# A hybrid SSM and convolution layer: SSM readout put into token order once by ScalarE, readout tables in three buffers, six weight low halves on VectorE

## The chip, the cores and the metric

The kernel runs on one core of a Trainium2 chip. The metric is device time in microseconds (us) of one execution, as the median of several executions. The engines are named as in the profile: PE is TensorE, PEld its weight load, DVE is VectorE, ACT is ScalarE, POOL is GpSimd, SP is the SyncE queue that issues most of the transfers.

## The reference

One layer of a diffusion backbone over 1024 latent tokens of 1024 channels, with a prefix of 256 context tokens. Cut to what the change touches:

```
p   = modulate(rmsnorm(x, norm1_g), sh1, sc1) @ w_in        # 512 SSM, 3 x 512 conv, 2 x 1024 gate columns
y   = d_skip * u + sum over 2 directions of Re(C @ states)  # S5 diagonal SSM, 32 groups of 16 channels, 64 states
z   = gelu(y)
y_a = z * sigmoid(z @ glu_w + glu_b)                        # GLU, 512 x 512
merged = sigmoid(p_a) * (y_a @ proj_a) + sigmoid(p_b) * (y_b @ proj_b)
x   = x + g1 * (merged @ w_out)
x   = x + g2 * conv_ffn(modulate(rmsnorm(x, norm2_g), sh2, sc2))   # g1, sh2, sc2, g2 from silu(c) @ mod_w
out = rmsnorm(x, final_g)
```

All tensors are float32.

## The kernel before

The large matrix products are made of three matmuls each: both operands are cut into a high half (a copy rounded to the PE's fp32r type) and a low half (operand minus high half), and high x high, low x high and high x low are summed in PSUM. `weight(src, lo_eng)` (L190) loads a weight tile of 128x1024 into `raw` (two buffers), ACT writes its high half `whi`, and `lo_eng`, POOL where `pool_e` is passed and DVE otherwise, writes the low half `wlo`. `split` (L205) does the same for activations: ACT the high half, DVE the low half. Each product that fills a 128x1024 PSUM tile is 48 matmuls of 128x512 for the gates (`gate_matmul`, key `ga` or `gb`) and 24 for the projections and the GLU (`proj_matmul`, keys `pa`, `pb`, `glu`). The PSUM tiles of this stretch rotate through two buffers, and ACT (a sigmoid, `sggb` or `sgga`) or DVE (`mb`, `sgga`) empties them.

The SSM works on chunks of 8 tokens: 128 latent chunks. Its readout for a pair of groups (`readout(sb)`, 16 of them) loads a table of three 128x128 matrices per group from `Yd` and the inputs of the two groups from `Ud` into one tile `wt` of two buffers, copies the chunk states out of `XS` into `S2` (ACT the upper 64 partitions, DVE the lower 64), multiplies, applies gelu into `Zt`, and stores `Zt` to `Zd`. `Zd` then holds z with the token index split as (place in the chunk j, chunk c). Four tiles `z[m]` are loaded from it in that order, 128 x 8 x 128. The high and low halves that the GLU and proj_a read are written in token order, so each `split` of a `z[m]` writes with a step of eight elements; the GLU's product with its sigmoid is done with the sigmoid read at that step.

Around the readouts run `branch_b(d)`, a gate `gb` and a product `pb` for each of 8 column blocks d. Then come the gate `ga0`, the four GLU products, and for each d a gate `ga` and a product `pa`. In the same stretch DVE works off 32 dot products for the second modulation (`mod_cols(n)`, tile `mw`, two buffers of 512 KB loads, result in `modc`), whose end the last scaled `w_out` tile and the norm of the second half wait for. Two small stores of `modc` columns (`mod_row`, into `rowd`) are in the SP queue as well.

The program is written once, and a scheduler orders the instructions of each engine ahead of time. Each engine, the SP queue too, works its list strictly in that order. A tile pool with n buffers lets the n+1st tile start only when the first one's last reader is done.

Of the kernel before, what the change touches and what calls it, by code (L numbers as in the profile page):

```python
# [13 lines left out]
F32 = mybir.dt.float32  # L14
# [3 lines left out]
AF = mybir.ActivationFunctionType  # L18
ALU = mybir.AluOpType
# [3 lines left out]
P = 128  # L23
D = 1024
SEQ = 1024
# [7 lines left out]
MS = SW // P  # L33
G = 32
H = 16
L = 8
NCC = CTX // L
NCL = SEQ // L
# [117 lines left out]
def layer_kernel(es: ExitStack, tc, I, out):  # L156
    nc = tc.nc
    sync, act, dve, pool_e, pe = nc.sync, nc.scalar, nc.vector, nc.gpsimd, nc.tensor

    def pool(name, bufs=1, stack=es, **kw):  # L160
        return stack.enter_context(tc.tile_pool(name=name, bufs=bufs, **kw))
# [17 lines left out]
    def ax_tile(shape, key):  # L179
        return psum["ax"].tile(shape, F32, name=f"ax_{key}", tag="ax")  # L180
# [3 lines left out]
    hold = {}  # L184

    def held(eng):
        ins = hold.get(eng)
        return tc.issue_after(ins.ins) if ins is not None else nullcontext()

    def weight(src, lo_eng=None, wpool=wp, scale=None):  # L190
        i = cnt["w"]
        cnt["w"] += 1
        raw = wp.tile([P, D], F32, name=f"raw{i}", tag="raw", bufs=2)
        sync.dma_start(raw, src)
        if scale is not None:
            dve.tensor_tensor(raw, raw, scale, op=ALU.mult)  # L196
        hi = wpool.tile([P, D], F32R, name=f"whi{i}", tag="whi")
        with held("act"):
            act.activation(hi, raw, AF.Copy)  # L199
        lo = wpool.tile([P, D], F32R, name=f"wlo{i}", tag="wlo")  # L200
        with held("dve") if lo_eng is None else nullcontext():
            (lo_eng or dve).tensor_tensor(lo, raw, hi.bitcast(F32), op=ALU.subtract)  # L202
        return hi, lo

    def split(hi, lo, src):  # L205
        act.activation(hi, src, AF.Copy)  # L206
        return dve.tensor_tensor(lo, src, hi.bitcast(F32), op=ALU.subtract)  # L207
# [23 lines left out]
    Ud = dram.tile([SW, L, NC], F32, name="Ud")  # L231
    NSB = G // 2
    Zd = dram.tile([MS, P, L, NCL], F32, name="Zd")
    Yd = dram.tile([NSB, P, 2, 3, P], F32, name="Yd")
# [168 lines left out]
    s, c = sm.sincos(sm.tt(li, dt, ALU.mult))  # L403
# [288 lines left out]
    conv = {}  # L692
# [80 lines left out]
    def ytile(key, m):  # L773
        return (yp.tile([P, SEQ], F32R, name=f"{key}h{m}", tag=f"yh{m}"),
                yp.tile([P, SEQ], F32R, name=f"{key}l{m}", tag=f"yl{m}"))
# [13 lines left out]
    rd = pool("rd", bufs=2, stack=es_x)  # L789

    def readout(sb):
        g0 = sb * 2
        wt = rd.tile([P, 2, 4, P], F32, name=f"wt{sb}", tag="wt")
        sync.dma_start(wt[:, :, 0:3, :], Yd[sb])
        sync.dma_start(wt[:, :, 3, :],
                       Ud[g0 * H:(g0 + 2) * H, :, NCC:].rearrange("(g h) j c -> (h j) g c", h=H))
        S2 = rd.tile([P, 2, 2, NCL], F32, name=f"S2{sb}", tag="S2")
        for i in range(2):
            src = XS[:, NCC - 1:NC - 1, i, g0:g0 + 2].rearrange("p s g -> p g s")
            act.activation(S2[0:64, i], src[0:64], AF.Copy)  # L800
            dve.tensor_copy(S2[64:128, i], src[64:128, :, ::-1])
        py = ax_tile([P, 2, NCL], f"Y{sb}")
        for g in range(2):
            pe.matmul(py[:, g, :], wt[:, g, 0, :], S2[:, 0, g, :], start=True, stop=False)
            pe.matmul(py[:, g, :], wt[:, g, 1, :], S2[:, 1, g, :], start=False, stop=False)
            pe.matmul(py[:, g, :], wt[:, g, 2, :], wt[:, g, 3, :], start=False, stop=True)
        Zt = rd.tile([P, 2, NCL], F32, name=f"Zt{sb}", tag="Zt")
        act.activation(Zt, py, AF.Gelu_apprx_tanh)
        for g in range(2):
            m, q = divmod(g0 + g, 8)  # L810
            sync.dma_start(Zd[m][q * H:(q + 1) * H].rearrange("h i c -> i h c"), Zt[:, g, :])

    def proj_matmul(wt, d, rh, rl, key):
        ps = mm_tile(key)
        hi, lo = wt
        for n in range(2):
            sl = slice(n * HALF, (n + 1) * HALF)
            for k in range(MS):
                ks = slice((d * MS + k) * P, (d * MS + k + 1) * P)
                mm3(ps[:, sl], (hi[:, ks], lo[:, ks]), (rh[k][:, sl], rl[k][:, sl]), k == 0, k == MS - 1)  # L820
        return ps

    def gate(m, key):
        psg = gate_matmul(m, key, None if 24 <= m < 28 else pool_e)
        sg = sgp.tile([P, SEQ], F32, name=f"sg{key}", tag="sg")
        act.activation(sg, psg, AF.Sigmoid)
        return sg
# [9 lines left out]
    for d, n in enumerate((0, 6, 6, 4)):  # L837
        branch_b(d)
        for q in range(n):
            readout(nread + q)  # L840
        nread += n
# [5 lines left out]
    mb += [mbt[1][:, d, :] for d in range(KT - MA)]  # L847
    es_z = ExitStack()
    zp = pool("zp", stack=es_z)
    z = [zp.tile([P, L, NCL], F32, name=f"z{m}") for m in range(MS)]  # L850
    for m in range(MS):
        sync.dma_start(z[m], Zd[m])
    es_md = ExitStack()
    md = pool("md", bufs=2, stack=es_md, side="right")
    sc2 = md.tile([P, D], F32, name="sc2", bufs=1)
# [3 lines left out]
    def mod_cols(n):  # L859
        mw = md.tile([P, D], F32, name=f"mw{n}", tag="mw")  # L860
        sync.dma_start(mw, I["mod_wT"][n * P:(n + 1) * P, :])
        with held("y"):
            dve.tensor_tensor_reduce(out=mw, in0=mw, in1=sc2, scale=1.0, scalar=0.0, op0=ALU.mult, op1=ALU.add,  # L863
                                     accum_out=modc[:, n:n + 1])
# [11 lines left out]
    def ysplit(key):  # L876
        hi, lo = [], []
        for m in range(MS):
            h, l_ = ytile(key, m)
            hold["y"] = split(h.rearrange("p (c j) -> p j c", j=L), l_.rearrange("p (c j) -> p j c", j=L), z[m])  # L880
            hi.append(h)
            lo.append(l_)
        return hi, lo

    zh, zl = ysplit("z")
    sgd = {0: gate(16, "ga0")}
    NM = 16 + 9 + 6
    for n in range(16 + 9, NM):
        mod_cols(n)
    for m in range(MS):  # L890
        if m % 2 == 0:
            wt = weight(I["glu_w"][m // 2], pool_e)
        ps = proj_matmul(wt, m % 2, zh, zl, f"glu{m}")
        sg = zp.tile([P, SEQ], F32, name=f"sgz{m}", tag="sgz", bufs=1)
        act.activation(sg, ps, AF.Sigmoid, bias=glub[:, m:m + 1])
        dve.tensor_tensor(z[m], z[m], sg.rearrange("p (c j) -> p j c", j=L), op=ALU.mult)
    yah, yal = ysplit("ya")

    def mod_done(a, b):
# [14 lines left out]
    def load_wout(k, src):  # L914
        raw = (wo.tile([P, D], F32, name=f"raw_o{k}", tag="xr", bufs=2) if k < 3 else
               wp.tile([P, D], F32, name=f"raw_o{k}", tag="raw", bufs=2))
        sync.dma_start(raw, I["w_out"][k * P:(k + 1) * P, :])
        (dve if k < 3 else pool_e).tensor_tensor(raw, raw, g1b, op=ALU.mult)
        hi, lo = (src.tile([P, D], F32R, name=f"wo{t}{k}", 
                          **({"tag": "sg"} if src is sgp else {"tag": f"y{t}{k % MS}", "bufs": 1})) for t in ("h", "l"))  # L920
        split(hi, lo, raw)
        wout.append((hi, lo))

    for d in range(KT):
        if d + 1 < KT:
            sgd[d + 1] = gate(17 + d, f"ga{d + 1}")
        if d % 2 == 0:
            wt = weight(I["proj_a"][d // 2], pool_e)
        ps = proj_matmul(wt, d % 2, yah, yal, f"pa{d}")
        sg = sgd.pop(d)  # L930
        dve.tensor_tensor(sg, ps, sg, op=ALU.mult)
        pool_e.tensor_tensor(mb[d], mb[d], sg, op=ALU.add)
        for n in range(NM + 5 * (d - 1), min(48, NM + 5 * d)) if d else ():
            mod_cols(n)
        if 2 <= d < 4:
            load_wout(d - 2, wo)
        if d == 5:
            es_md.close()
            md = pool("md2", stack=es_g, side="right")
            load_wout(2, md)  # L940
# [5 lines left out]
    op = pool("op", bufs=2, stack=es_o)  # L946
# [81 lines left out]
    f = [fp.tile([P, SEQ], F32, name=f"f{k}") for k in range(KF)]  # L1028
# [183 lines left out]
```

## Time and profile before

| what | value |
|---|---|
| runs, us | 1459.26, 1464.06, 1464.45 |
| median of the three, us | 1464.06 |
| profiled execution, own time, us | 1457.23 |
| profiled execution, span, us | 1455.4 |
| PE busy in the span | 1399.7 us (96%) |
| DVE, ACT, POOL busy | 979.1, 535.2, 477.5 us |
| granted PE clock over the span, mean | 0.987 |

The profiled execution is a little faster than the three timed ones; 1.8 us of its own time lie outside the span. Matmuls are pipelined, so a matmul's duration is longer than the distance to the next one, and PE counts as busy also while it works at its lower clock. The readouts lie between 354 and 421 us of the span, the GLU between 458 and 487, and the gates and products with proj_a reach to about 617.

### The profile page before, as it was taken

The page shows a single profiled execution, that of the slowest core. Times are in us where ns is not written, and L with a number is a line of the kernel's source. Part 1 is how long each engine was busy: PE and PEld are TensorE (multiplying, and loading weights), DVE is VectorE, ACT ScalarE, POOL GpSimd, SP SyncE. Part 2 cuts the span into 40 slices and gives each one's busy share as a digit, 9 for nine tenths or more (in the row PEclk, how much of TensorE's full clock was granted, in tenths as well). Part 3 has the DMA queues.
Part 4 walks back from the last instruction along what each step waited for, and adds up shares of the span by engine and source line. Part 5 has one row for each costly group of instructions (what it writes and reads, how often), then busy time and mean ns, then how long its engine had stood idle before and what let it go on. Part 6 is the DMA issues. An engine that isn't in the chain of part 4 may idle for free. (4 is left out here: it accounts for less than half of the span.)

```text
span 1455.4 us, 16944 instructions
## 1 busy us (share of the span) xinstructions
PE 1399.7 (96%) x6488; PEld 1144.0 (79%) x6488; DVE 979.1 (67%) x1424; ACT 535.2 (37%) x758; POOL 477.5 (33%) x211
## 2 busy tenths in 40 slices
PE   6999989999899999999999999999999999998997
PEld 4788877788787777878888888888888887887885
DVE  6865859888227782147568877877878886349555
ACT  5643772223434411135433332332332342324332
POOL 0000000002101334340055465465465465635453
PEclk9999999999989999999999999999999999999998
DMA  9613212512677474143111111111111115424331
GB/s 323 208 52 96 80 57 74 143 44 87 191 236 164 154 236 103 32 143 108 71 45 58 44 46 57 44 47 55 44 50 52 44 58 188 145 87 156 100 106 58
DMA packets 82577, 148.71 MB, mean 102 GB/s; under 512 B 22336, under 2 KB 51264, under 8 KB 82496
## 3 DMA queue, kind: packets, MB, share of 16 engines
q1 hardware_dynamic: 79616, 137.90, 31.1%
q10 hardware_dynamic: 2880, 9.73, 1.9%
q8 instruction: 51, 0.84, 0.2%
q14 instruction: 30, 0.25, 0.1%
HBM read 129.80 MB, written 19.90 MB: 103 GB/s over the span
## 5 line engine op out<-in xcount | busy, mean ns | idle before, releaser
L202 POOL TENSOR_TENSOR wlo<-raw,whi 128x1024 fp32r<-128x1024 f32 x108 | 269.8, 2502 | 758.6 <-ACT whi L199 750.9
L1052 DVE SCALAR_TENSOR_TENSOR acc<-mm_up,cw,acc 128x945 f32<-128x945 f32 (+2 forms) x308 | 375.0, 1223 | 100.4 <-POOL acc L1044 91.6
L199 ACT ACTIVATE whi<-raw 128x1024 fp32r<-128x1024 f32 x126 | 133.6, 1060 | 535.4 <-issue 192.5
L213 PE MATMUL mm_up<-h2hi,wlo 128*128 128x512 f32 x704 | 274.0, 389 | 0.5 <-POOL wlo L202 0.5
L211 PE MATMUL mm_up<-h2hi,whi 128*128 128x512 f32 x704 | 273.7, 389 | 0.4 <-DVE h2hi L987 0.4
L212 PE MATMUL mm_up<-h2lo,whi 128*128 128x512 f32 x704 | 274.1, 389 | 0.0
L213 PEld LDWEIGHTS mm_up<-h2hi,wlo 128*128 128x128 f32 x704 | 132.2, 188 | 28.2 <-POOL wlo L202 0.9
L211 PEld LDWEIGHTS mm_up<-h2hi,whi 128*128 128x128 f32 x704 | 132.1, 188 | 27.9 <-DVE h2hi L987 0.7
L212 PEld LDWEIGHTS mm_up<-h2lo,whi 128*128 128x128 f32 x704 | 132.2, 188 | 27.6
L211 PE MATMUL mm_dn<-whi,fhd 128*128 128x512 f32 x308 | 119.5, 392 | 6.0 <-DVE x1r L1140 4.5
L212 PE MATMUL mm_dn<-wlo,fhd 128*128 128x512 f32 x308 | 120.6, 392 | 2.5 <-POOL wlo L202 2.5
L213 PE MATMUL mm_dn<-whi,fld 128*128 128x512 f32 x308 | 120.2, 391 | 0.0
L1044 POOL TENSOR_TENSOR acc<-acc,side 128x960 f32<-128x960 f32 x44 | 100.4, 2281 | 0.0
L207 DVE TENSOR_TENSOR fld<-f,fhd 128x512 fp32r<-128x512 f32 x44 | 58.6, 1347 | 52.4 <-ACT fhd L206 52.4
L863 DVE CUSTOM_DVE_ANT_0 mw<-mw,sc 128x1024 f32<-128x1024 f32 x32 | 54.2, 1706 | 43.0 <-DMA mw<-in_mod_wT_dram 25.5
L211 PEld LDWEIGHTS mm_dn<-whi,fhd 128*128 128x128 f32 x308 | 58.2, 189 | 19.0 <-DVE x1r L1140 4.9
L212 PEld LDWEIGHTS mm_dn<-wlo,fhd 128*128 128x128 f32 x308 | 58.3, 189 | 15.3 <-POOL wlo L202 3.5
L213 PEld LDWEIGHTS mm_dn<-whi,fld 128*128 128x128 f32 x308 | 58.1, 189 | 12.1
L196 DVE TENSOR_TENSOR raw<-raw,g2b 128x1024 f32<-128x1024 f32 x22 | 42.8, 1947 | 34.9 <-DMA raw<-in_ffn_w_down_dram 34.9
L1063 POOL TENSOR_TENSOR f<-f,acc 128x1024 f32<-128x1024 f32 x22 | 53.3, 2424 | 10.0 <-DVE acc L1052 10.0
L213 PE MATMUL mm_ga<-hhi,wlo 128*128 128x512 f32 x128 | 50.7, 396 | 4.1 <-POOL wlo L202 4.1
L213 PE MATMUL mm_o<-woh,ml 128*128 128x512 f32 x128 | 50.8, 398 | 1.1 <-DVE ml L207 1.1
(324 smaller groups left out, 2646.8 us busy)
## 6 DMA issues: line engine op xcount, KB each, us to landing
raw<-in_ffn_w_up_dram SPq DMA_DIRECT2D x44, 512.0 KB
raw<-in_ffn_w_down_dram SPq DMA_DIRECT2D x44, 512.0 KB
mw<-in_mod_wT_dram SPq DMA_DIRECT2D x32, 512.0 KB
raw<-in_w_in_dram SPq DMA_DIRECT2D x28, 512.0 KB
wt<-Yd SPq DMA_DIRECT2D x16, 384.0 KB
mt<-in_mod_wT_dram SPq DMA_DIRECT2D x8, 512.0 KB
mn<-in_mod_nat_dram SPq DMA_DIRECT2D x8, 512.0 KB
Yd<-W SPq DMA_DIRECT2D x16, 256.0 KB
```

Source lines behind the costliest of these rows:

```text
L196: dve.tensor_tensor(raw, raw, scale, op=ALU.mult)
L199: act.activation(hi, raw, AF.Copy)
L202: (lo_eng or dve).tensor_tensor(lo, raw, hi.bitcast(F32), op=ALU.subtract)
L207: return dve.tensor_tensor(lo, src, hi.bitcast(F32), op=ALU.subtract)
L211: pe.matmul(ps, lh, rh, start=first, stop=False)
L212: pe.matmul(ps, lh, rl, start=False, stop=False)
L213: pe.matmul(ps, ll, rh, start=False, stop=last)
L863: dve.tensor_tensor_reduce(out=mw, in0=mw, in1=sc2, scale=1.0, scalar=0.0, op0=ALU.mult, op1=ALU.add, accum_out=modc[:, n:n + 1])
L1044: pool_e.tensor_tensor(acc[:, 1:, :], acc[:, 1:, :], side[:, 1:, :], op=ALU.add)
L1052: dve.scalar_tensor_tensor(acc[:, r0:r1, c0:c1], u[:, r0 + dr:r1 + dr, c0 + dc:c1 + dc], cw[:, m, i:i + 1], acc[:, r0:r1, c0:c1], op0=ALU. ...
L1063: pool_e.tensor_tensor(f[k], f[k], v, op=ALU.mult)
```

## The change

```diff
     def readout(sb):
         g0 = sb * 2
-        wt = rd.tile([P, 2, 4, P], F32, name=f"wt{sb}", tag="wt")
-        sync.dma_start(wt[:, :, 0:3, :], Yd[sb])
-        sync.dma_start(wt[:, :, 3, :],
-                       Ud[g0 * H:(g0 + 2) * H, :, NCC:].rearrange("(g h) j c -> (h j) g c", h=H))
+        wt = rd.tile([P, 2, 3, P], F32, name=f"wt{sb}", tag="wt", bufs=3)
+        sync.dma_start(wt, Yd[sb])
+        if sb % 2 == 0:
+            ut = rd.tile([P, 4, NCL], F32, name=f"ut{sb}", tag="ut")
+            sync.dma_start(ut, Ud[g0 * H:(g0 + 4) * H, :, NCC:].rearrange("(g h) j c -> (h j) g c", h=H))
+            conv["ut"] = ut
+        ut = conv["ut"]
...
-            pe.matmul(py[:, g, :], wt[:, g, 2, :], wt[:, g, 3, :], start=False, stop=True)
+            pe.matmul(py[:, g, :], wt[:, g, 2, :], ut[:, sb % 2 * 2 + g, :], start=False, stop=True)
...
-    z = [zp.tile([P, L, NCL], F32, name=f"z{m}") for m in range(MS)]
+    z = [zp.tile([P, SEQ], F32, name=f"z{m}") for m in range(MS)]
     for m in range(MS):
-        sync.dma_start(z[m], Zd[m])
+        zj = zp.tile([P, L, NCL], F32, name=f"zj{m}", tag="zj", bufs=2)
+        sync.dma_start(zj, Zd[m])
+        act.activation(z[m].rearrange("p (c j) -> p j c", j=L), zj, AF.Copy)
...
-            hold["y"] = split(h.rearrange("p (c j) -> p j c", j=L), l_.rearrange("p (c j) -> p j c", j=L), z[m])
+            hold["y"] = split(h, l_, z[m])
...
-            wt = weight(I["glu_w"][m // 2], pool_e)
+            wt = weight(I["glu_w"][m // 2])
...
-        dve.tensor_tensor(z[m], z[m], sg.rearrange("p (c j) -> p j c", j=L), op=ALU.mult)
+        dve.tensor_tensor(z[m], z[m], sg, op=ALU.mult)
...
-            wt = weight(I["proj_a"][d // 2], pool_e)
+            wt = weight(I["proj_a"][d // 2])
```

The table of a readout is now one contiguous run per partition and has three buffers; the inputs come for two readouts at once in a tile of their own with two buffers. The four z tiles are loaded into `zj` (two buffers) and copied by ACT into token order, after which every reader reads and writes them in one run. The low halves of two GLU and four proj_a weight tiles go from POOL to DVE. No matmul is added or removed.

The scheduler's order changes with it. On PE, before, 115 matmuls of 128x512 lie between the first matmul of the first readout and the last of the last; now there are 68, and the last readout stands ahead of `pb5` instead of inside `gb6`, so that 216 matmuls follow it up to the GLU, where before 168 did.

In the SP queue, the end of the readouts before. `wt` rows with Yd load a table, those with Ud the inputs of the same readout; Zd rows store a result, in two transfers each:

```order
L794 DMA wt13_3380<-Yd_90 128x2x384
L795 DMA wt13_3380<-Ud_88 128x2x128
L811 DMA Zd_89<-Zt11_3274 8x16x128 x2
L794 DMA wt14_3399<-Yd_90 128x2x384
L795 DMA wt14_3399<-Ud_88 128x2x128
L811 DMA Zd_89<-Zt12_3376 8x16x128 x2
L794 DMA wt15_3418<-Yd_90 128x2x384
L811 DMA Zd_89<-Zt13_3395 8x16x128 x2
L795 DMA wt15_3418<-Ud_88 128x2x128
```

The same place in the SP queue now, `ut` being the inputs for two readouts:

```order
L794 DMA wt11_3260<-Yd_90 128x768
L814 DMA Zd_89<-Zt8_3218 8x16x128 x2
L794 DMA wt12_3361<-Yd_90 128x768
L797 DMA ut12_3363<-Ud_88 128x4x128
L814 DMA Zd_89<-Zt9_3236 8x16x128 x2
L794 DMA wt13_3381<-Yd_90 128x768
L814 DMA Zd_89<-Zt10_3256 8x16x128 x2
L794 DMA wt14_3399<-Yd_90 128x768
```

The table of readout n stood behind the store of readout n-2 or n-3; it now stands behind that of n-4, and inputs no longer stand behind a store that is needed for nothing in front of them.

On ACT, what follows the last readout before (`Zt15` is its gelu, `sc2` the silu of c for the dot products, `zh` the high halves for the GLU):

```order
L808 ACTIVATE Zt15_3433<-ax_Y15_3426 128x256
L199 ACTIVATE whi29_3741<-raw29_3739 128x1024
L826 ACT_TABLE_LOAD
L826 ACTIVATE sggb6_3699<-mm_gb6_3650 128x1024
L857 ACT_TABLE_LOAD
L857 ACTIVATE sc2_3457<-sc2_3457 128x1024
L199 ACTIVATE whi30_3856<-raw30_3854 128x1024
L826 ACT_TABLE_LOAD
L826 ACTIVATE sggb7_3794<-mm_gb7_3745 128x1024
L206 ACTIVATE zh0_3838<-z0_3446 128x8x128
```

And on ACT now:

```order
L811 ACT_TABLE_LOAD
L811 ACTIVATE Zt15_3433<-ax_Y15_3426 128x256
L199 ACTIVATE whi28_3711<-raw28_3709 128x1024
L857 ACTIVATE z0_3446<-zj0_3450 128x8x128
L857 ACTIVATE z1_3447<-zj1_3453 128x8x128
L862 ACT_TABLE_LOAD
L862 ACTIVATE sc2_3465<-sc2_3465 128x1024
L857 ACTIVATE z2_3448<-zj2_3456 128x8x128
L857 ACTIVATE z3_3449<-zj3_3459 128x8x128
L199 ACTIVATE whi29_3749<-raw29_3747 128x1024
L829 ACT_TABLE_LOAD
L829 ACTIVATE sggb6_3707<-mm_gb6_3658 128x1024
```

The four copies into token order, and the silu among them, stand ahead of the high half `whi29` that `gb7` multiplies with and of the sigmoid `sggb6` that empties the PSUM buffer into which `gb7` is summed.

On DVE, around the low halves `zl` for the GLU before (an ISA row is a dot product, or the read of its sum):

```order
L863 ISA mw24_3828,modc_82<-mw24_3828,sc2_3457 128x1024
L863 ISA modc_82 128x1
L207 TENSOR_TENSOR zl0_3839<-z0_3446,zh0_3838 128x8x128
L834 TENSOR_TENSOR mb1_3442<-mm_pb7_3796,sggb7_3794 128x1024
L207 TENSOR_TENSOR zl1_3843<-z1_3447,zh1_3842 128x8x128
L207 TENSOR_TENSOR zl2_3847<-z2_3448,zh2_3846 128x8x128
L207 TENSOR_TENSOR zl3_3851<-z3_3449,zh3_3850 128x8x128
L863 ISA mw25_3911,modc_82<-mw25_3911,sc2_3457 128x1024
```

And on DVE now, with the first GLU low half `wlo31` that POOL had:

```order
L868 ISA mw24_3836,modc_82<-mw24_3836,sc2_3465 128x1024
L868 ISA modc_82 128x1
L207 TENSOR_TENSOR zl0_3847<-z0_3446,zh0_3846 128x1024
L837 TENSOR_TENSOR mb1_3442<-mm_pb7_3804,sggb7_3802 128x1024
L207 TENSOR_TENSOR zl1_3851<-z1_3447,zh1_3850 128x1024
L207 TENSOR_TENSOR zl2_3855<-z2_3448,zh2_3854 128x1024
L202 TENSOR_TENSOR wlo31_3941<-raw31_3937,whi31_3939 128x1024
L207 TENSOR_TENSOR zl3_3859<-z3_3449,zh3_3858 128x1024
```

The same nine dot products are ahead of `zl0` as before; the four low halves keep their places, in one run each, with a weight's low half among them.

## Rows read from the trace of the kernel before

**Rows 1.** The page, part 1: busy time, share of the span, instructions.
```profile
PE 1399.7 (96%) x6488; PEld 1144.0 (79%) x6488; DVE 979.1 (67%) x1424; ACT 535.2 (37%) x758; POOL 477.5 (33%) x211
```

**Rows 2.** Windows: length, busy us (instructions) per engine, granted clock, DMA share, GB/s.
```profile
395.00:400.00 5.00, 2.24 (x18) 2.08 (x19) 1.11 (x2) 1.43 (x3) 1.60 (x1) 1.00 0.84 248
400.00:410.00 10.00, 9.02 (x39) 7.89 (x38) 2.41 (x6) 4.29 (x9) 0.00 (x0) 0.51 0.60 166
420.00:455.00 35.00, 35.00 (x154) 28.67 (x154) 14.20 (x19) 18.47 (x14) 7.15 (x3) 1.00 0.71 226
461.70:468.50 6.80, 5.91 (x14) 3.70 (x13) 5.64 (x5) 1.97 (x2) 1.71 (x1) 0.50 0.72 179
560.60:564.00 3.40, 3.40 (x9) 2.63 (x10) 0.00 (x0) 0.00 (x0) 3.40 (x2) 0.51 0.67 27
```

**Rows 3.** Waits of PE, 350 to 640 us: total us, times, longest.
```profile
PE mm_ga L213 <- POOL wlo L202: 4.1, 2, 3.2
PE ax_Y L804 <- DMA wt<-Yd: 2.9, 2, 2.7
PE mm_glu L212 <- DVE zl L207: 2.8, 3, 2.0
PE mm_pa L213 <- POOL wlo L202: 2.1, 1, 2.1
```

**Rows 4.** PE timeline, one readout's first row and the next one's.
```profile
375.55 0.38 PE L804 MATMUL ax_Y<-S,wt 128*128 128x128 f32 x2
...
376.89 0.39 PE L804 MATMUL ax_Y<-S,wt 128*128 128x128 f32 x2
```

**Rows 5.** Tile wt: first matmuls of all readouts, ns, first and last start.
```profile
L804 PE MATMUL ax_Y<-S,wt x64: 270/275/551, 358.7 to 419.0; 128*128 128x128 f32 x64
```

**Rows 6.** SP queue timeline: start, issue time, transfer.
```profile
404.19 0.56 SPq L794 DMA_DIRECT2D wt<-Yd  x1
404.79 0.60 SPq L795 DMA_DIRECT2D wt<-Ud  x1
405.49 1.19 SPq L811 DMA_DIRECT2D Zd<-Zt  x2
...
420.26 1.21 SPq L811 DMA_DIRECT2D Zd<-Zt  x2
423.43 0.33 SPq L852 DMA_DIRECT2D z<-Zd  x1
...
481.08 19.65 SPq L194 DMA_DIRECT2D raw<-in_w_in_dram  x2
```

**Rows 7.** ACT timeline, after the readouts.
```profile
426.43 1.28 ACT L826 ACT_TABLE_LOAD   x1
...
430.38 1.06 ACT L857 ACTIVATE sc<-sc 128x1024 f32<-128x1024 f32 x1
...
445.50 6.22 ACT L206 ACTIVATE zh<-z 128x1024 fp32r<-128x1024 f32 x3 [0.27 <-PE mm_pb L213]
```

**Rows 8.** DVE timeline, 450 to 560 us.
```profile
452.80 3.35 DVE L863 CUSTOM_DVE_ANT_0 mw<-mw,sc 128x1024 f32<-128x1024 f32 x1 [1.21 <-DMA mw<-in_mod_wT_dram]
...
459.27 5.91 DVE L207 TENSOR_TENSOR zl<-z,zh 128x1024 fp32r<-128x1024 f32 x3
...
519.28 1.21 DVE L863 CUSTOM_DVE_ANT_0 mw<-mw,sc 128x1024 f32<-128x1024 f32 x1
...
553.15 0.18 DVE L900 TENSOR_TENSOR modc<-modc,modk 128x24 f32<-128x24 f32 x1
```

**Rows 9.** Tile raw on DVE: the low halves that DVE makes already, min/median/max ns.
```profile
L202 DVE TENSOR_TENSOR wlo<-raw,whi x18: 1215/1220/1227, 61.5 to 325.5; 128x1024 fp32r<-128x1024 f32 x18
```

**Rows 10.** POOL timeline: low halves beside DVE's work.
```profile
452.65 2.42 POOL L202 TENSOR_TENSOR wlo<-raw,whi 128x1024 fp32r<-128x1024 f32 x1 [7.29 <-ACT whi L199]
...
494.68 5.69 POOL L202 TENSOR_TENSOR wlo<-raw,whi 128x1024 fp32r<-128x1024 f32 x1 [15.14 <-ACT whi L199]
...
558.08 4.66 POOL L202 TENSOR_TENSOR wlo<-raw,whi 128x1024 fp32r<-128x1024 f32 x2
```

## The prediction

> **What bounds the kernel now.** I read the page first. PE is busy 96% of the span and no other engine over 67% [rows 1], so a change that adds or removes no matmul can gain only what PE loses: idle time, and time at its lower clock. The profiled execution took 1457.2 us, 6.8 under the median of the runs shown; the sums go against 1457.2.
>
> Next I read the waits of PE in the stretch that the change touches [rows 3], then the windows around them for the clock [rows 2]. At full clock 154 matmuls of 128x512 go through in 35.00 us, 0.227 us each [rows 2]. A readout repeats after 376.89 − 375.55 = 1.34 us when nothing holds it up [rows 4]. PE's losses by these two prices:
>
> - Readouts: the first starts at 358.7 and the last reaches its end some 0.7 us after 419.0 [rows 5], so 61.0 us; 16 readouts and the 115 other matmuls in between need 16 x 1.34 + 115 x 0.227 = 47.5. **13.5 us** are lost. The waits for tables are 2.9 of it [rows 3]. After a stretch in which PE was busy 2.24 of 5.00 us, the granted clock stood at 0.51 for the 10 us from 400 to 410 (the 1.2 GHz level), which is some 5 more [rows 2].
> - Start of the GLU: 2.8 of waits for `zl` [rows 3], and 6.80 us at 0.50 with 5.91 busy, half of which is lost [rows 2]: **5.8**.
> - First `pa`: 2.1 waiting for POOL's `wlo` [rows 3], a pass that took 5.69 us beside DVE [rows 10]: **2.1**.
> - `ga` products: 4.1 in two waits [rows 3], and 3.40 us at 0.51, half lost [rows 2]: **5.8**.
>
> Together 27.2 us. Elsewhere the change alters nothing.
>
> **The change, part by part.** *Tables and inputs.* The SP queue issues a readout's table in 0.56 us, inputs in 0.60, and the result in 1.19, 2.35 together [rows 6]; now inputs come half as often, and if one transfer for four groups issues in 0.60 to 1.20, a readout costs 2.05 to 2.35. What goes is the order: a table stood behind the store of readout n−2 or n−3, and a store waits for a gelu; it now stands behind n−4, with a third buffer to land in. PE's own work between first and last readout falls to 16 x 1.34 + 68 x 0.227 = 36.9 us, or 2.3 per readout. So PE and the SP queue now want the same time each, and DMA is not far off: a readout moves 0.39 MB of table, 0.13 of inputs and 0.13 of result, 0.65 MB, which at 248 GB/s (share 0.84 [rows 2]) is 2.6 us, and at full share, 295 GB/s, 2.2. The loss lies between 1 us (one first wait) and 16 x 0.8 = 12.8, if each readout takes 3.1 us, that is 2.35 of issue and 0.75 of waiting behind a store. Three tables let loads run ahead of the stretch, and the 48 us of DMA work need not all fall into it; I take 3.5, nearer the lower end, since only 2.9 of 13.5 were table waits before. Gain 13.5 − 3.5 = **10.0**. The 47 matmuls that leave the stretch only move behind it.
>
> *Copies by ACT.* Four copies of 128x1024 are added, reading in one run and writing at a step. The nearest rows are `zh`, 6.22 for three, 2.07 each, at the same step [rows 7], and 1.06 for a pass in one run [rows 7]. I take 2.07, 8.3 in all. With T the end of the last readout on PE: its gelu lies behind a table load, of 1.28 [rows 7], and part of `sggb5`: T+3.1 (from T+1.7 to T+4.0). The store is issued in 1.21 [rows 6]: T+4.3. Before, the first load of z followed the end of its issue by 423.43 − 421.47 = 2.0 [rows 6], so `zj0` goes out at T+6.3; I let it land 3.4 later (2.0 as for the store, to 4.1 with 512 KB at 248 GB/s added): T+10. `z0`, `z1`: T+14.1. Table load and silu, 1.28 + 1.06: T+16.5. `z2`, `z3`: T+20.6. `whi29`, 1.06: T+21.7; table load and `sggb6`, 2.34: T+24.1. Until then `gb7` cannot start. PE reaches it after `pb5`, `gb6` and `pb6`, 24 + 48 + 24 = 96 matmuls: T+21.8. A new stall of **2.3**, then; with copies at 1.06 none, with late landings 6, and should the clock fall as it did after the waits above, 1.7 to 3 more. I put half a microsecond for that: 2.8 in all.
>
> *GLU start.* PE reaches the GLU after 216 matmuls: T + 49.0 + 2.3 = T+51.3, which I call G. DVE still has nine dot products ahead of `zl0`. Before, the ninth began at 452.80 [rows 8], T+33 (T = 419.7). The silu they need ended at T+11.7 [rows 7] and now ends 5 later, so `zl0` starts by about T+39.5. A `zl` in one run I price as DVE's `wlo`, 1.22 [rows 9], against 5.91/3 = 1.97 before [rows 8]. Four, the merge `mb1` and `wlo31`, also 1.22 each: T+47, 4 before G. The 5.8 go. If the queue shifts by 8 instead of 5, the last `zl` is still in time, since the first suffices at G.
>
> *Low halves on DVE.* Six passes at 1.22 [rows 9] stand in DVE's list. The first `pa` is wanted after 144 more matmuls, G+32.7. Behind the four GLU products (96 matmuls, G+21.8) lie a sigmoid, the product with z, `yah` and `yal`, one pass of 1.1 to 1.2 each in one run, with `wlo` among them: about G+26. The 2.1 go, with 6 to spare. The raw loads that stood in the SP queue from 481.08 for 19.65 us [rows 6] waited for buffers that POOL's pass held until 500.4 [rows 10]; at G+26 instead of 42.6 after that start they come 16 earlier, and the dot products behind them with them.
>
> *End of the dot products.* Before, they ended at 553.15 [rows 8], 95 after PE reached the GLU (T + 168 x 0.227 = 457.8). From this go up to 16 for the queue, and less if their loads pace them: I take 75 to 79. `sgga`, POOL's merge and its `wlo` (1.2 + 2.4 + 2.4) follow: G+81 to G+85. PE wants that `wlo` at the start of `ga5`, behind four GLU products, `ga1` to `ga4` and `pa0` to `pa3`: 96 + 4 x 72 = 384 matmuls, G+87. Before, POOL made two such halves in a row there, 4.66 [rows 10], one of which is now DVE's. So the 5.8 of the `ga` products go too, with the thinnest margin, 2 to 6.
>
> **Sum.** 1457.2 − 10.0 + 2.8 − 5.8 − 2.1 − 5.8 = 1436.3. The three runs shown lie 2.0 to 7.2 above the profiled one; adding some 4 for a median, **1440 us**.
>
> **Rivals.**
> *A, the readouts still starve.* SP and DMA are as loaded as PE. At 3.1 us each, as above, the stretch loses 12.8 instead of 3.5: 1440 + 9.3 = 1449. For it speaks a DMA share of 0.84 just where PE was busy 45% [rows 2]; against it, that tables were waited for only twice [rows 3]. Chance 0.18.
> *B, POOL catches DVE's new passes.* Dot products took 3.35 us beside a POOL pass and 1.21 alone [rows 8, 10]. Six low halves at the first figure cost 12.8 more on DVE, beyond the margin of 2 to 6, and the wait at `ga5` with its clock stays: 1440 + 5 = 1445. Chance 0.15. The Trainium skill has a rule for it ("SBUF — State Buffer", section "Who interferes with whom"): a DVE instruction with two inputs in SBUF contends with a GpSimd instruction that reads SBUF, under an exclusive lock. The 3.35 against 1.21 agrees; by the rule each new pass is exposed, though six POOL passes fewer are there to meet.
> *C, ACT's copies cost more.* The stall at 6 with 3 us of lost clock: 1440 + 6 = 1446. Chance 0.1.
> *D, slower than before: the packed readouts run at the lower clock.* Between readouts stand only four matmuls; a wait in each could hold the clock at 0.51, as from 400 to 410 [rows 2]. If it held through all 36.9 us of work, that work would take 74, 33 more than the 40.4 forecast: 1473. It decides once 48 us pass at that level, since half of it outweighs the gain of 24. Against it, the level lasted 10 us before. Chance 0.04. The Trainium skill ("TensorE: Matmul & The Clock Gate", section "HAM oscillation — how this bites in real kernels") describes a kernel whose short bursts between DMA waits started cold each time; in this trace one such wait had that effect in the readouts and others did not.
> *E, nothing comes of it:* the same DMA traffic paces readouts and dot products, and what PE gains it waits away at `gb7` and `ga5`: 1457 to 1464. Chance 0.05.
>
> **How the numbers follow.** The forecast holds 0.48. 0.5% is about what a measurement of this kernel can tell: under 1456.7 is faster, over 1471.4 slower. Forecast, B, C and nearly all of A are faster, 0.86; the worst of A and E are the same, 0.10; D is slower, 0.04. The range goes from 1430 (losses of 1 in the readouts and no stall give a sum of 1431, so that the runs start there) to 1454 (A with C's stall and a little): what is left out is E, D and a little below.
>
> **What the next profile would show.** Right: first to last readout in 37 to 42 us without a window at the lower clock; waits `mm_glu` for `zl`, `mm_pa` and `mm_ga` for `wlo` gone; a new wait of PE at `mm_gb` for ACT of about 2; `zl` and `wlo` on DVE at 1.2; the end of the dot products 71 to 79 after the GLU's start. Wrong: table or store waits in every readout (A), `wlo` on DVE near 3 and a wait at `ga5` (B), a stall before `gb7` of 5 or more (C), clock windows at 0.5 in the readouts (D).

## The result and the profile after

The changed kernel's median is 1437.95 us (1435.53 to 1440.69, 4 runs), against 1461.66 for the kernel before (1456.77 to 1464.45, 4 runs): a ratio of 0.984 with a 95% interval of 0.980 to 0.988. Run once more beside the experiments it gave 0.988 (0.986 to 0.990). The profiled execution has a span of 1433.7 and its own time 1435.53, where the prediction's sum was 1436.3.

Part 1 of the page after, which answers to [rows 1]:

```profile
PE 1391.4 (97%) x6488; PEld 1138.8 (79%) x6488; DVE 973.8 (68%) x1430; ACT 534.4 (37%) x761; POOL 459.0 (32%) x205
```

The waits of PE from 340 to 640 us, to set against [rows 3]:

```profile
PE mm_gb L211 <- ACT sggb L829: 4.3, 1, 4.3
PE ax_Y L807 <- DMA wt<-Yd: 3.1, 3, 1.3
PE ax_Y L807 <- DVE S L804: 0.2, 1, 0.2
```

The waits at `mm_glu`, `mm_pa` and `mm_ga` are gone, and a new one stands at `mm_gb`, for ACT. Windows over the readouts, over the new wait and behind it (columns as in [rows 2]):

```profile
356.80:398.60 41.80, 38.43 (x261) 34.28 (x261) 13.66 (x29) 24.90 (x47) 4.09 (x2) 1.00 0.80 239
420.50:424.90 4.40, 0.14 (x1) 0.00 (x0) 1.38 (x3) 4.34 (x4) 2.29 (x1) 0.82 0.68 223
424.90:430.10 5.20, 5.18 (x12) 3.73 (x13) 4.41 (x5) 0.00 (x0) 1.05 (x1) 0.50 0.75 247
```

The readouts take 41.8 us instead of 61.0, at full clock and with 36.9 of work: 4.9 us lost. PE then stands for 4.3 us, and the 5.2 us behind it run at 0.50 (the 1.2 GHz level), half of which is lost. No other window from `gb0` (278.8) to the second half (693.5) has a lowered clock. ACT's timeline shows what PE waited for:

```profile
401.72 0.39 ACT L811 ACTIVATE Zt<-ax_Y 128x256 f32<-128x256 f32 x1
403.92 1.06 ACT L199 ACTIVATE whi<-raw 128x1024 fp32r<-128x1024 f32 x1 [1.81 <-PE mm_pb L212]
411.08 4.14 ACT L857 ACTIVATE z<-zj 128x1024 f32<-128x1024 f32 x2 [6.09 <-DMA zj<-Zd]
415.23 1.28 ACT L862 ACT_TABLE_LOAD   x1
416.53 1.06 ACT L862 ACTIVATE sc<-sc 128x1024 f32<-128x1024 f32 x1
417.50 4.18 ACT L857 ACTIVATE z<-zj 128x1024 f32<-128x1024 f32 x2
421.48 1.05 ACT L199 ACTIVATE whi<-raw 128x1024 fp32r<-128x1024 f32 x1
422.55 1.28 ACT L829 ACT_TABLE_LOAD   x1
423.84 1.02 ACT L829 ACTIVATE sggb<-mm_gb 128x1024 f32<-128x1024 f32 x1
```

The sigmoid that frees the PSUM buffer of `gb7` has four copies and the silu ahead of it, and ACT itself stood 6.09 us for the first load of z. VectorE's and the queue's rows for that stretch:

```profile
448.99 1.22 DVE L207 TENSOR_TENSOR zl<-z,zh 128x1024 fp32r<-128x1024 f32 x1
...
536.48 0.18 DVE L905 TENSOR_TENSOR modc<-modc,modk 128x24 f32<-128x24 f32 x1
```
```profile
403.43 0.40 SPq L194 DMA_DIRECT2D raw<-in_w_in_dram  x1
405.13 0.80 SPq L856 DMA_DIRECT2D zj<-Zd  x2
```

The last `zl` ends at 450.2, 4.8 us before the GLU starts (455.0), and the dot products end 81.5 us after that start.

To compare places, one length serves below: from the first matmul of `gb0` to the first of the second half, by the tile views (**stretch**). It was 432.0 us before (280.6 to 712.6) and 414.7 after (278.8 to 693.5), or 415.3 when the changed kernel ran again. So the change is worth about 17 us; the medians of the changed kernel run again and of the kernel before beside it lie 18.1 apart. The other 4 of the first profile's 21.7 us (1457.23 − 1435.53) lie outside: 1.8 ahead of `gb0` (280.6 against 278.8) and 2.6 in the last products (`mm_dn` took 244.8 us before and 242.2 after). The kernel itself run again had 280.4 and 244.8 there, so this is scatter of the execution.

### The profile page after: what moved, and what is told of

The parts are those of the page before. It is cut to its first block, busy times and chain, and to the rows that moved or that the text cites. A ratio compares the mean times of both kernels' runs of the same rounds, so it can differ in the third digit from the quotient of the medians.

```text
span 1433.7 us, 16945 instructions
## 1 busy us (share of the span) xinstructions
PE 1391.4 (97%) x6488; PEld 1138.8 (79%) x6488; DVE 973.8 (68%) x1430; ACT 534.4 (37%) x761; POOL 459.0 (32%) x205
## 5 line engine op out<-in xcount | busy, mean ns | idle before, releaser
L202 POOL TENSOR_TENSOR wlo<-raw,whi 128x1024 fp32r<-128x1024 f32 x102 | 251.5, 2468 | 759.1 <-ACT whi L199 756.9
L211 PE MATMUL mm_dn<-whi,fhd 128*128 128x512 f32 x308 | 119.1, 391 | 3.2 <-DVE x1r L1145 3.2
L868 DVE CUSTOM_DVE_ANT_0 mw<-mw,sc 128x1024 f32<-128x1024 f32 x32 | 45.0, 1411 | 41.0 <-DMA mw<-in_mod_wT_dram 28.5
L212 PEld LDWEIGHTS mm_dn<-wlo,fhd 128*128 128x128 f32 x308 | 58.1, 189 | 15.4 <-POOL wlo L202 3.5
L213 PEld LDWEIGHTS mm_dn<-whi,fld 128*128 128x128 f32 x308 | 58.2, 189 | 12.1
L211 PE MATMUL mm_gb<-hhi,whi 128*128 128x512 f32 x128 | 51.5, 402 | 4.3 <-ACT sggb L829 4.3
L213 PE MATMUL mm_gb<-hhi,wlo 128*128 128x512 f32 x128 | 51.7, 404 | 0.0
```

What stands on the lines that cost most here:

```text
L211: pe.matmul(ps, lh, rh, start=first, stop=False)
L212: pe.matmul(ps, lh, rl, start=False, stop=False)
L213: pe.matmul(ps, ll, rh, start=False, stop=last)
```

## The experiments

Ratios are to the kernel before, run beside each. The changes of the stretch are against 432.0; each is read from one profiled execution, so a us or two between them tells little, and where stretch and ratio disagree the ratio counts.

| kernel | ratio (95%) | stretch, us |
|---|---|---|
| changed, again | 0.988 (0.986 to 0.990) | −16.7 |
| without the tables | 0.998 (0.996 to 0.999) | −2.1 |
| without the copies | 0.990 (0.988 to 0.992) | −12.1 |
| without the low halves on VectorE | 0.989 (0.987 to 0.990) | −15.4 |
| tables alone | 0.990 (0.988 to 0.992) | −13.3 |
| third buffer alone | 0.991 (0.989 to 0.993) | −10.1 |
| copies alone | 0.996 (0.994 to 0.997) | −4.5 |
| low halves alone | 0.998 (0.997 to 0.999) | +0.5 |
| changed, copies on GpSimd | 0.984 (0.982 to 0.986) | −22.0 |
| the same, and `gb7`'s low half on VectorE | 0.986 (0.984 to 0.988) | −17.0 |
| copies on GpSimd, written later | 0.985 (0.983 to 0.987) | −19.5 |
| without the tables, row store in runs (see below) | 0.991 (0.989 to 0.993) | −11.9 |

**The parts taken out one at a time.** First the tables:

```diff
-        wt = rd.tile([P, 2, 3, P], F32, name=f"wt{sb}", tag="wt", bufs=3)
+        wt = rd.tile([P, 2, 4, P], F32, name=f"wt{sb}", tag="wt")
...
```

> The changed kernel with the readout tables and inputs of before (one tile for both, two buffers); copies into token order and the low halves on VectorE stay. Its order has 114 other matmuls between the first and last readout again, and only the first copy ahead of the high half and the sigmoid that the seventh gate waits for. My theory: the readouts lose about 13.5 us again instead of 4.9, the 4.3 us wait of the seventh gate and its stretch at the lower clock go (6.9 together), and the waits at the GLU, pa and ga stay away, so it ends 1 to 3 us above the changed kernel, a ratio to before of 0.984 to 0.989. Rival, the tables carry the change and the rest is small: 8 us or more above the changed kernel, 0.990 or more. Rival, the copies land late without the packed readouts: a wait at the GLU for zl or zh of 2 us or more.

The theory fell: the first rival's number held, by another way than it said. The readouts took 60.9 us again, and a wait of a new kind came at the GLU. VectorE's timeline of that kernel:

```profile
461.70 1.22 DVE L865 CUSTOM_DVE_ANT_0 mw<-mw,sc 128x1024 f32<-128x1024 f32 x1
462.84 0.09 DVE L865 DVE_READ_ACCUMULATOR2_ANT modc<- 128x1 f32 x1
474.44 3.21 DVE L865 CUSTOM_DVE_ANT_0 mw<-mw,sc 128x1024 f32<-128x1024 f32 x1 [11.51 <-DMA mw<-in_mod_wT_dram]
477.58 0.08 DVE L865 DVE_READ_ACCUMULATOR2_ANT modc<- 128x1 f32 x1
477.58 1.22 DVE L202 TENSOR_TENSOR wlo<-raw,whi 128x1024 fp32r<-128x1024 f32 x1
```

and the wait that this makes on PE:

```profile
PE mm_glu L213 <- DVE wlo L202: 8.5, 2, 7.9
```

The low half stands in VectorE's list behind a dot product whose load took until 474.44, and PE waits 7.9 us for it. On GpSimd it had no such neighbour.

Next, without the copies (`split` writes its halves, and the product reads the sigmoid, at a step again):

```diff
-        act.activation(z[m].rearrange("p (c j) -> p j c", j=L), zj, AF.Copy)
...
-            hold["y"] = split(h, l_, z[m])
+            hold["y"] = split(h.rearrange("p (c j) -> p j c", j=L), l_.rearrange("p (c j) -> p j c", j=L), z[m])
...
```

> The changed kernel without the copies into token order: z is loaded, split and multiplied at a step of eight elements as before; tables and low halves stay as changed. My theory of the prediction (strided low halves make the GLU late) expects the wait at the GLU for zl back, 2.8 us and a stretch at the lower clock, 5.8 us in all, while the wait of the seventh gate goes (6.9 us): about 1 us under the changed kernel, ratio 0.983 to 0.985. The rival that I now hold likelier: with the readouts packed, PE reaches the GLU 49 us after the last readout instead of 38, which is enough for strided passes as well; then no wait at the GLU, no wait at the seventh gate, and it is some 7 us faster than the changed kernel, ratio about 0.980. A third: the strided passes push the low halves behind them, and a wait at pa or ga of 1 to 3 us comes back.

The waits of PE there:

```profile
PE mm_pa L213 <- DVE wlo L202: 2.3, 2, 1.3
PE mm_pa L211 <- ACT yah L206: 2.3, 1, 2.3
PE ax_Y L807 <- DMA wt<-Yd: 1.9, 2, 1.7
PE mm_pa L212 <- DVE yal L207: 1.6, 1, 1.6
PE mm_ga L213 <- POOL wlo L202: 1.3, 1, 1.3
```

There is no wait at `mm_glu`, nor at `mm_gb` for ACT: the strided passes for the GLU are in time once PE reaches it 50.6 us after the last readout's start instead of 38.8. Up to the GLU this kernel is 6.1 us ahead of the changed one (50.6 against 56.7). But it gives that back and more behind it, at `pa`: from the first `pa` to the first `mm_o` it takes 121.4 us, against 110.5. So what the copies pay they pay at the y passes, not at the GLU. The net is another matter: this profiled execution (1445.65) lies 4.4 us above its kernel's median, and by the medians, 1441.21 against 1440.26 for the changed kernel run again, the copies' net worth beside the other two parts is not shown; they also bring the stall at `gb7`. Of my three expectations the third came nearest, with too small a size.

Then the low halves back on GpSimd:

```diff
-            wt = weight(I["glu_w"][m // 2])
+            wt = weight(I["glu_w"][m // 2], pool_e)
...
```

> The changed kernel with the six low halves (two GLU, four proj_a weight tiles) back on GpSimd. My theory: the waits at pa (2.1 us) and ga (4.1 us and a low-clock stretch of 1.7) come back, some 8 us, ratio 0.989 to 0.990. Rival: these waits came from the late GLU and from strided passes and stay away, and the time is that of the changed kernel within 2 us, ratio 0.983 to 0.986.

The rival holds in its mechanism. The waits at `pa` and `ga` come to 1.4 us in all instead of 6.2 in [rows 3], and the median, 1440.6, is that of the changed kernel run again. The ratio, 0.989, is not the one that the rival named, since the changed kernel's own came out at 0.988 the second time:

```profile
PE mm_gb L211 <- ACT sggb L829: 4.4, 1, 4.4
PE mm_ga L213 <- POOL wlo L202: 1.4, 2, 0.9
```

**The parts put in alone.**

> The kernel before with the readout part of the change alone: tables in three buffers, inputs for four groups; no copies, low halves on GpSimd. Its order has 67 other matmuls between the first and last readout. My theory now: the tables carry most of the change, because the readouts lose some 4 instead of 13.5 us and the GLU, 49 us behind the last readout, finds its strided low halves ready, so that 8.6 and 5.8 us go; waits at pa and ga of some 8 us with their clock stay. Some 10 to 14 us faster than before, ratio 0.990 to 0.993. Rival (the prediction's): the late GLU comes from the strided passes and stays; then 8 us, 0.994 or more, and a wait at the GLU for zl of 2 us or more.

The readouts took 39.3 us, and no wait for `zl` is left at the GLU. My new theory holds, and the prediction's reason for that wait falls: cured by order, not by contiguous passes. A GpSimd low half is late there instead, so that the GLU products still take 25.9 us, against 28.3 before and 22.2 in the changed kernel:

```profile
PE mm_ga L213 <- POOL wlo L202: 3.4, 2, 2.2
PE mm_glu L213 <- POOL wlo L202: 2.1, 1, 2.1
PE mm_pa L213 <- POOL wlo L202: 1.8, 1, 1.8
```

The third buffer alone is one word of the kernel before:

```diff
-        wt = rd.tile([P, 2, 4, P], F32, name=f"wt{sb}", tag="wt")
+        wt = rd.tile([P, 2, 4, P], F32, name=f"wt{sb}", tag="wt", bufs=3)
```

> The kernel before with nothing but a third buffer for its readout tile, whose inputs are still loaded with each table. The order is packed (67 other matmuls among the readouts) by this alone. Theory: the third buffer is what the gain in the readouts comes from; within 2 us of the variant with the whole readout part, ratio 0.990 to 0.994. Rival: the inputs loaded half as often carry it, since PE and the queue want the same time for a packed readout; then the readouts take 46 us or more instead of 42, with waits for tables or inputs in most of them and perhaps the lower clock, and it is 4 us or more behind that variant.

It gives 0.991 against 0.990. By the readouts, 42.8 us from the first to the last start against 39.3, the inputs loaded half as often may be worth 3 us; the ratios' intervals overlap. In the same group of runs the whole change gave 18.1 us by the medians, and this one word 13.1.

> The kernel before with the copies into token order on ScalarE alone; tables as before, low halves on GpSimd. Theory: the wait at the GLU for zl goes (5.8 us) and contiguous passes take the waits at pa and ga down from 8.5 us in all to 2 to 6, against 1.4 us at the seventh gate: 5 to 10 us faster than before, ratio 0.993 to 0.997. Rival: GpSimd's low halves make the GLU late instead, a wait of 3 us or more at mm_glu for wlo, and it is within 3 us of before.

0.996, as the theory had it, but not by its way. The last readout is late again, and 2.5 us of waiting for `zl` are left at the GLU although the passes are contiguous. At `pa` the wait for a GpSimd low half is gone; at `ga` 3.9 of the 4.1 us of [rows 3] stay:

```profile
PE mm_ga L213 <- POOL wlo L202: 3.9, 2, 3.2
PE mm_glu L212 <- DVE zl L207: 2.5, 1, 2.5
```

> The kernel before with the six low halves on VectorE alone; tables and strided passes as before. Theory: VectorE works its list in order, and the second GLU low half stands behind dot products whose loads come late after the small store of modulation columns, as in the variant with the old tables (a wait of 7.9 us at the GLU with a stretch at the lower clock behind it); this eats what the waits at pa and ga give (8 us). Between 3 us faster and 3 us slower than before, ratio 0.998 to 1.002, with a wait of 5 us or more at mm_glu for wlo. Rival (the prediction's): the waits at pa and ga go and nothing comes for them, 7.9 us faster, ratio about 0.9945.

0.998, inside the theory's range, though not by its way: the wait at the GLU is 3.4 us where 5 or more were expected, and the low half stands there behind two strided `zl`, not behind a late load. The prediction's price of 7.9 us for this part fails, as nothing is left of it when the part is put in alone; waits of VectorE's own making take the place of those for GpSimd:

```profile
PE mm_glu L213 <- DVE wlo L202: 3.4, 1, 3.4
PE mm_pa L213 <- DVE wlo L202: 2.8, 1, 2.8
PE mm_pa L212 <- DVE yal L207: 1.6, 1, 1.6
```

**What held VectorE 11.5 us.** In the kernel without the tables a store of 1024 single numbers of `modc` goes out at 458.40, just ahead of the late loads. The edit stores them in another order, so this kernel's output is not the layer's; it serves only to time the store:

```diff
-        sync.dma_start(rowd[i].rearrange("(k p) -> p k", p=P), modc[:, n * KT:(n + 1) * KT])
+        sync.dma_start(rowd[i].rearrange("(p k) -> p k", p=P), modc[:, n * KT:(n + 1) * KT])
```

> The variant with the old tables (copies and low halves as changed), with one more edit: the two small stores of modulation columns write 8 neighbouring numbers of each partition in one run instead of single 4-byte numbers. That puts the row g1 (and g2) into DRAM in another order of its columns, so the residual is scaled with permuted columns; the amount of work is the same. Theory: the 11.5 us in which VectorE waited for a dot product's load there came from that store's 1024 single numbers in the transfer engines; with 128 short runs the wait for the second GLU low half (7.9 us) and the lower clock behind it shrink to 2 us or less, 8 to 10 us faster than that variant, ratio 0.990 to 0.992. Rival: the loads are late because of their place in the SP queue; the wait stays above 5 us, ratio 0.996 to 0.999.

The theory holds: 9 us faster than the kernel without the edit, by the medians (1445.12 against 1454.24) and 9.8 by the stretch, with 1.6 us of waiting left at the GLU. Windows of the kernel without the edit, the store within the first:

```profile
459.00:464.00 5.00, 4.44 (x19) 3.61 (x20) 3.93 (x6) 1.34 (x2) 0.00 (x0) 1.00 0.27 9
464.00:469.00 5.00, 5.00 (x24) 4.03 (x23) 0.00 (x0) 1.12 (x1) 0.00 (x0) 1.00 0.95 39
```

and with it, where the store was issued at 460.69:

```profile
459.00:464.00 5.00, 3.45 (x15) 2.55 (x14) 5.00 (x8) 1.97 (x2) 0.00 (x0) 1.00 0.44 147
464.00:469.00 5.00, 5.00 (x23) 3.96 (x23) 2.90 (x6) 1.12 (x1) 0.00 (x0) 1.00 0.74 251
```

At a share of 0.95 the transfer engines moved 39 GB/s behind the single numbers, and 251 GB/s at 0.74 without them.

**The new wait at `gb7`.**

```diff
-        act.activation(z[m].rearrange("p (c j) -> p j c", j=L), zj, AF.Copy)
+        pool_e.tensor_copy(z[m].rearrange("p (c j) -> p j c", j=L), zj)
```

> The changed kernel with the four copies into token order on GpSimd instead of ScalarE, where the order then has the high half and the sigmoid for the seventh gate with no copy ahead of them. My theory (the 4.3 us wait of the seventh gate comes from the copies' place on ScalarE, and the low clock behind it follows from the wait): the wait and the stretch at the lower clock go, 6.9 us, ratio about 0.980, if GpSimd needs no more than about 5 us for a copy. Rival: the wait comes from the late landing of the readouts' results, and a wait of 2 us or more stays at the seventh gate. Rival: a strided copy on GpSimd takes 8 us or more, and the wait moves to the GLU or to low halves that stand behind the copies, ratio 0.984 or more.

The theory holds in its mechanism: the wait for ACT and the lower clock behind it are gone. Its size does not (5.3 us of stretch instead of 6.9, ratio 0.984 instead of 0.980). The median, 1434.41, is the lowest of the study. GpSimd needs as long for a copy as ACT (2.14 to 2.21 for three of the four, against 2.15 to 2.27 on ACT); the third took 3.16. What is left is a wait of 1.6 us, as `gb7`'s low half stands behind that third copy, which is what the last rival said would follow from slow copies:

```profile
413.28 2.21 POOL L857 COPY z<-zj 128x1024 f32<-128x1024 f32 x1
416.41 3.16 POOL L857 COPY z<-zj 128x1024 f32<-128x1024 f32 x1 [0.92 <-DMA zj<-Zd]
419.41 2.36 POOL L202 TENSOR_TENSOR wlo<-raw,whi 128x1024 fp32r<-128x1024 f32 x1
```

Two attempts to take this wait away made it longer. In the first the low half goes to VectorE:

```diff
-        psg = gate_matmul(m, key, None if 24 <= m < 28 else pool_e)
+        psg = gate_matmul(m, key, None if 24 <= m < 28 or m == 31 else pool_e)
```

> The changed kernel with the copies into token order on GpSimd, and with the low half of the seventh gate's weight on VectorE, since on GpSimd it stood behind the third copy and made PE wait 1.65 us. Theory: that wait goes, 1.8 us faster than the variant with the copies on GpSimd alone, 6 to 8 us faster than the changed kernel, ratio 0.981 to 0.983. Rival: VectorE reaches the low half late, behind dot products that wait for their loads, and a wait of 2 us or more stands at the seventh gate again.

The rival holds, 3.3 us:

```profile
419.32 3.05 DVE L868 CUSTOM_DVE_ANT_0 mw<-mw,sc 128x1024 f32<-128x1024 f32 x1
422.30 0.08 DVE L868 DVE_READ_ACCUMULATOR2_ANT modc<- 128x1 f32 x1
423.09 1.22 DVE L868 CUSTOM_DVE_ANT_0 mw<-mw,sc 128x1024 f32<-128x1024 f32 x1 [0.71 <-DMA mw<-in_mod_wT_dram]
424.24 0.08 DVE L868 DVE_READ_ACCUMULATOR2_ANT modc<- 128x1 f32 x1
424.24 1.22 DVE L202 TENSOR_TENSOR wlo<-raw,whi 128x1024 fp32r<-128x1024 f32 x1
```

In the second the loop of loads and copies stands behind `branch_b(7)` in the code (`zcopy(m)`, the same three lines):

```diff
...
+    for m in range(MS):
+        zcopy(m)
     es_ps.close()
```

> The changed kernel with the copies into token order on GpSimd and written behind the last gate and product of branch b, so that on GpSimd the seventh gate's low half stands ahead of the third copy. Theory: neither ScalarE nor GpSimd holds the seventh gate up any more: no wait above 0.5 us from the last readout to the dot products' end and full clock throughout, about 7 us faster than the changed kernel and 1 to 2 faster than the variant with the copies on GpSimd alone, ratio 0.982 to 0.984. Rival: the later loads of z make the high and low halves for the GLU late, a wait of 1 us or more at the GLU.

Neither theory nor rival: the GLU is in time, but z is now loaded behind two loads for dot products, and the first two copies, and with them the low half, come later (417.72 for the first, where it was 408.95), a wait of 3.2 us:

```profile
417.72 4.96 POOL L857 COPY z<-zj 128x1024 f32<-128x1024 f32 x2 [8.71 <-DMA zj<-Zd]
422.50 3.26 POOL L202 TENSOR_TENSOR wlo<-raw,whi 128x1024 fp32r<-128x1024 f32 x1
```

The changed kernel as the yardstick:

> The changed kernel once more, as the yardstick on the chip and beside the runs of before of this group. From its own runs a ratio to before of 0.980 to 0.988 is known; with the parts measured one by one I expect 0.984 to 0.988, 4 to 6 us above the variant with the copies on GpSimd, and the 4.3 us wait of the seventh gate again.

It is 5.3 us of stretch behind the kernel with the copies on GpSimd (415.3 against 410.0), with the 4.4 us wait at `gb7` again.

## Why the prediction was right, and which of its steps were not

The time, its sign and the bound (PE's losses and nothing else) came out as forecast. Of the rivals only C came near: the stall cost 6.9 us, between the 2.8 of the forecast and C's 9. The parts, one by one:

- **Readouts**: 41.8 us of 40.4 forecast, 4.9 lost instead of 3.5. The step holds, and the run with the third buffer alone shows which edit does it: it lets the scheduler pack the readouts, 67 or 68 other matmuls between the first and the last instead of 115. The gain is 8.6 us where 10.0 were forecast.
- **Copies by ACT**: the mechanism was right, its size off: a wait of 4.3 and 2.6 us of lost clock, 6.9 where 2.8 were forecast. PE came to `gb7` at T+21.9 (T, the end of the readouts, is now 398.6), as computed; the sigmoid ended at T+26.3 instead of T+24.1. Two terms failed, by 2 us each. One is the clock, for which I put 0.5 and which took 2.6. The other is the landing of the first z. Issued at 405.13, near the T+6.3 of the forecast, it was on hand only at 411.08, 5.95 us later, where I took 3.4 with 4.1 as the upper bound. Everything behind it on ACT took as long as computed. What the landing goes with is what went out just ahead. In the changed kernel a weight load of 512 KB was issued 1.7 us before the first z (at 403.43), as in four more kernels, and in these five z took 4.7 to 5.95 us to land. In the three kernels with the old tables and the copies the weight load stood 8.3 us ahead, and z took 3.5. The prediction priced the load as if it went alone. (Its row for the start, the load of z at 423.43, was also not the first of z but the fourth; the first three had gone out at 415.00.)
- **GLU start**: the 5.8 us went. The prediction counted them under contiguous passes, and that step is wrong: the wait for `zl` goes with the tables alone, because PE comes to the GLU later after the readouts, and it stays with the copies alone. What the tables alone leave there, a late GpSimd low half, goes with either of the other two parts: without the copies, and with the low halves on GpSimd, the GLU products took 22.2 us too. The prediction's own terms would have shown it: at 1.97 instead of 1.22 for each `zl`, 3 us more, the last is ready at about T+50, still ahead of G. That `zl` kept its margin (4.8 us, 4 forecast) is partly luck: `zl` and PE both came about 5 us later than computed.
- **Low halves on VectorE**: the 7.9 us for `pa` and `ga` went, but with the low halves left on GpSimd they go too, all but 1.4 us of waits, and put in alone the low halves bring 4.4 us of waiting for VectorE at `pa` in exchange. The step that failed is the one that hung these waits on GpSimd: beside the other two parts it does not matter which engine makes the low half. The contiguous y passes carry most of this term: without the copies `pa` to `mm_o` takes 11 us longer. They do not carry it alone: with the copies by themselves it took 116.9 us, with the copies and either of the other parts 110.6 and 112.2 (119.1 before). Why the wait at `ga` needs a second part was not tried.
- **End of the dot products**: 81.5 us after the GLU's start instead of 71 to 79. The margin held, since no wait is left at `ga5`, but it is as thin as feared: run again, the changed kernel waited 0.4 us for a GpSimd low half at a `ga`. Rival B has no support: all of VectorE's low halves took 1.21 to 1.23 us.
- That the sum came out within 1 us (1436.3 against 1435.53) is luck. The forecast gain was 20.9 us and the stretch gave 17.3: the stall took 4 more and the readouts gave 1.4 less, while the GLU and the products behind it gave some 2 more. The 4 us of scatter in the profile ahead of and behind the stretch made up for it. Its parts do not add either: alone they give 13.3, 4.5 and −0.5 us of stretch, together 17; pairs differ again (the copies and the low halves without the tables give 2.1).

## What to carry to other kernels

A buffer count is an edit to the order: one more buffer, a single word, let the scheduler pack the readouts and gave 13.1 of the 18.1 us, and that moved every deadline behind them, so that waits which seemed to belong to slow passes went as well. Before a wait is credited to an edit, ask whether the edit that moves the waiting engine's arrival removes it too. A pass moved to another engine takes over that engine's queue: here a low half behind dot products had to wait for their loads, and a copy ahead of a sigmoid held up PE. In each case the place in the list decided, not the 1 or 2 us of the pass.

## What the runs showed of the hardware

A store of 1024 single 4-byte numbers slowed the loads beside it for about ten microseconds (39 GB/s at a share of 0.95), and cost 9 us of kernel time where a compute engine stood behind those loads. The kernel before has the same store, issued at 451.84, and from 460 to 464 us its transfer engines moved 39 GB/s at a share of 0.92. The changed kernel has it too, at 438.35, where PE waited for nothing; whether storing in runs would help that kernel was not tried.

Two stalls of PE of nearly the same length had different ends. After the 3.3 us in the kernel with the low half on VectorE the clock was at 0.50 for the next 5.2 us, and after the 3.2 us in the kernel with the later copies it stayed at 1.00:

```profile
425.50:430.70 5.20, 5.19 (x12) 4.17 (x13) 2.21 (x3) 0.00 (x0) 2.07 (x1) 0.50 1.00 376
```
```profile
425.80:430.80 5.00, 4.99 (x22) 4.11 (x23) 2.65 (x5) 0.00 (x0) 3.10 (x1) 1.00 0.72 256
```

What sets these two apart was not tried. The two kernels' stretches differ by 2.5 us (−17.0 and −19.5), about the half that is lost of 5.2, so a stall's price can nearly double with it. The length of the wait alone does not decide it: behind the 2.1 us wait at the GLU in the kernel with the tables alone (PE went on at 449.96) the clock fell as well:

```profile
452.00:455.00 3.00, 3.00 (x9) 2.39 (x8) 0.91 (x2) 1.97 (x2) 0.94 (x1) 0.55 0.96 365
```
